# An MLP's first stage by seven products instead of eight, through DRAM, in a hybrid decoder block

## The chip, the cores and the metric

The kernel runs on one core of a Trainium2 chip. The metric is the device time of one execution in microseconds (us); lower is better. A core has TensorE (PE, matrix products; its weight loads are listed apart as PEld), VectorE (DVE), ScalarE (ACT), GpSimd (POOL) and SyncE (SP), which here issues all transfers between DRAM and the on-chip memory SBUF. Products land in PSUM, eight banks of 128 x 512 floats.

## The reference

One decoder layer over 2048 tokens of width 1024 in float32. Attention and a gated spatial mixer come first; the change touches the MLP behind them:

```python
h = _rmsnorm(x, norm_pre_mlp[layer])
a = jax.nn.relu(jnp.einsum('bsd,df->bsf', h, w_mlp_in[layer]))   # 1024 -> 4096
y = jnp.einsum('bsf,fd->bsd', a * a, w_mlp_out[layer])           # 4096 -> 1024
x = x + _rmsnorm(y, norm_post_mlp[layer])
```

## The kernel before, in words

**Precision.** Every large product is made of three matmuls. `split` (L68 to L76) turns a float32 tile into a high part, rounded to the matmul's type (on ACT, L71, or POOL, L73), and a low part, the rest (DVE, L76). `mm3` (L85 to L88) multiplies high by high, high by low and low by high into one PSUM bank. `split_in` (L78 to L83) loads by SP and then splits.

**Order.** PE's order is written out by hand (`tc.manual_schedule`, L57): it executes matmuls in the order of the program. The queues of the other engines are put in order by the framework's scheduler, from priorities in program order and when inputs are ready; each engine then executes its queue in order. SP's queue holds all transfers and is in order too: one that waits holds up those behind it. A pool of tiles with `bufs=n` under one `tag` lets a new tile be written once the n-th older one has been read for the last time.

**Before the MLP.** `out_block` (L762) works on 128 tokens: output projection, residual, two norms, and in its second part, which `flush` (L806) runs one block later, transposes of the normed rows (L799) that ACT copies (L800) and SP writes to the DRAM tensor `h2_d` (L801), laid out depth by token. The token chunks of 512 go in the order 2, 3, 0, 1, so the upper half (`half` 1) is ready first, and the MLP begins with it. The last blocks of out_block, those of chunk 1, belong to half 0. While their last flush is still to come, PE has the first two stage-1 tiles of half 1 (two calls of `mlp_in`).

**The MLP.** For each half of 1024 tokens, f runs over 32 tiles of 128 hidden channels.

- Stage 1, `mlp_in` (L842): for one f and one chunk of 512 tokens, 8 depth tiles x 3 = 24 matmuls into one bank (`a`). ACT takes the relu out of the bank (L854), POOL squares it (L855), and ACT and DVE split it into the tile `s` that stage 2 uses from SBUF.
- Weights: `load_w1` and `load_w2` load 512 KB for each f, POOL makes the high part and DVE the low one.
- Stage 2, `mlp_out` (L913): for a group of FG = 2 tiles f it goes over 8 token blocks i and 2 column halves n; each (i, n) is 2 x 3 matmuls into a bank (`y`), which DVE adds to the accumulator in SBUF (L932). A group is made up one step behind stage 1. The last group of a half takes 4 f and goes on to the final norm: ACT squares (L935), POOL multiplies by the gain (L936), DVE ends the norm (L938, `rstd_of` L90 to L104) and adds the residual (L943), SP writes the output.

Both stages alternate on PE inside one loop over f. `psum_any` deals out all eight banks in turn to `a` and `y`.

Of the kernel before, what the change touches and what calls it, by code (L numbers as in the profile page):

```python
# [8 lines left out]
F32 = mybir.dt.float32  # L9
F32R = mybir.dt.float32r  # L10
AF = mybir.ActivationFunctionType
# [5 lines left out]
P = 128  # L17
S = 2048
D = 1024
KT = 8  # L20
NF = 32
# [3 lines left out]
HALF = 1024  # L25
FG = 2
# [16 lines left out]
def block_kernel(ctx, tc, a, out):  # L43
    nc = tc.nc
    pe, act, dve, pool, sp = nc.tensor, nc.scalar, nc.vector, nc.gpsimd, nc.sync
    x = a["x"]

    def stack(es, name, bufs=1, side=None, space=None):
        kw = dict(name=name, bufs=bufs, reuse_waits="tile")
        if side:  # L50
            kw["side"] = side
        if space is not None:
            kw["space"] = space
        return es.enter_context(tc.tile_pool(**kw))
# [13 lines left out]
    def split(hi, lo, src, hi_eng="act", lo_eng="dve"):  # L68

        if hi_eng == "act":  # L70
            act.activation(hi, src, AF.Copy)  # L71
        elif hi_eng == "pool":
            pool.tensor_scalar(hi, src, 1.0, 1.0, op0=OP.mult, op1=OP.mult)  # L73
        else:
            dve.tensor_copy(hi, src)
        (pool if lo_eng == "pool" else dve).tensor_sub(lo, src, f32(hi))  # L76

    def split_in(w, src, raw=None, hi_eng="pool", lo_eng="dve"):  # L78

        if raw is None:  # L80
            raw = f32(w)[:, 1]
        sp.dma_start(raw, src)
        split(w[:, 0], w[:, 1], raw, hi_eng, lo_eng)  # L83

    def mm3(ps, lh, ll, rh, rl, start, stop):  # L85
        pe.matmul(ps, lh, rh, start=start, stop=False)  # L86
        pe.matmul(ps, lh, rl, start=False, stop=False)  # L87
        pe.matmul(ps, ll, rh, start=False, stop=stop)  # L88
# [18 lines left out]
    def dtile(shape, name):  # L107
        return dram.tile(shape, F32, name=name)
# [9 lines left out]
    yg_d = dtile([4, P, S], "ygd")  # L118
    x1_d = dtile([S, D], "x1d")
    h2_d = dtile([P, KT, S], "h2d")  # L120
    hT_d = dtile([2, P, KT, 512], "hTd")


# [157 lines left out]
    with ExitStack() as e1a:  # L281
# [6 lines left out]
        for n in range(2):  # L288
            p = psum_aux(f"busy{n}")
# [29 lines left out]
        for half in range(2):  # L319
# [343 lines left out]
    for n in range(len(units) + 1):  # L663
        u = None
# [144 lines left out]
            last[0] = None  # L809

    chunks = (2, 3, 0, 1)
    e3 = ExitStack()
    s_, w1_, w2_, hch, cnt, raws, rls = {}, {}, {}, {}, [0], {}, []
# [5 lines left out]
    def load_h(half, ci):  # L819
        if (half, ci) in hch:  # L820
            return
        c = half * 2 + ci
        h = (hB if ci else r3).tile([P, 2, KT, 512], F32R, name=f"h2T{c}", tag="h2T", bufs=1)
        for k in range(0, KT, 2):
            split_in(h[:, :, k:k + 2], h2_d[:, k:k + 2, c * 512:(c + 1) * 512], None, "act")
        hch[half, ci] = h

    def load_w1(half, f):
        if (half, f) not in w1_:
            w1_[half, f] = r3.tile([P, 2, KT, P], F32R, name=f"w1_{half}{f}", tag="w1", bufs=2)  # L830
            if (half, f) in raws:
                raw = raws.pop((half, f))
            else:
                raw = wp3.tile([P, KT, P], F32, name=f"w1r_{half}{f}", tag="wraw", bufs=2)
            split_in(w1_[half, f], a["w_mlp_in"][f], raw)

    def load_w2(half, f):
        w2_[half, f] = wp3.tile([P, 2, D], F32R, name=f"w2_{half}{f}", tag="w2", bufs=4)
        raw = wp3.tile([P, D], F32, name=f"w2r_{half}{f}", tag="wraw", bufs=2)
        split_in(w2_[half, f], a["w_mlp_out"][f], raw)  # L840

    def mlp_in(half, f, ci):  # L842

        nm = f"{half}{f}{ci}"
        h, w1 = hch[half, ci], w1_[half, f]
        if ci == 0 and f % 4 < 2:
            s = r3.tile([P, 2, 512], F32R, name=f"s_{nm}", tag="s", bufs=2)
        else:
            s = sL.tile([P, 2, 512], F32R, name=f"s_{nm}", tag="s")
        p = psum_any(f"a_{nm}")  # L850
        for k in range(KT):
            mm3(p, w1[:, 0, k, :], w1[:, 1, k, :], h[:, 0, k, :], h[:, 1, k, :], k == 0, k == KT - 1)
        t = rls.pop() if rls else tp3.tile([P, 512], F32, name=f"rl_{nm}", tag="rl", bufs=2)
        act.activation(t, p, AF.Relu)  # L854
        pool.tensor_mul(t, t, t)  # L855
        split(s[:, 0], s[:, 1], t)
        s_[half, f, ci] = s

    def spatial_out(dt):

# [17 lines left out]
    for n, c in enumerate(chunks):  # L878
        if n:
            mg = merge(c, yt, {2: flush})  # L880
        if n < 3:
            yt = load_y(chunks[n + 1])
        for i in range(4):
            b = out_block(c, i, mg)
            next(b)
            flush()
            last[0] = b
            if n == 3 and i == 1:
                e2r.close()
                r3 = stack(e3, "r3", 1, side="right")  # L890
                load_h(1, 0)
                rw = yp.tile([P, 3, KT, P], F32, name="w1r_first", tag="yt")
                for f in range(2):
                    raws[1, f] = rw[:, f]
                    rls.append(rw[:, 2, f * 4:(f + 1) * 4].rearrange("p k t -> p (k t)"))
                    load_w1(1, f)


    first_half, second_half = 1, 0
    for f in range(2):  # L900
        mlp_in(first_half, f, 0)
    flush()
    e2.close()
    wp3 = stack(e3, "wp3", 1)
    hB = stack(e3, "hB", 1)
    yp = stack(e3, "yp3", 1)
    sL = stack(e3, "sL", 6)
# [5 lines left out]
    def mlp_out(half, f0, n_f, acc):  # L913
        first, final = f0 == 0, f0 + n_f == NF
        for i in range(8):
            isl = slice((i % 4) * P, (i % 4 + 1) * P)
            t0 = half * HALF + i * P
            if final:
                x1 = tp3.tile([P, D], F32, name=f"x1_{half}{i}", tag="x1", bufs=3)
                sp.dma_start(x1, x1_d[t0:t0 + P, :])  # L920
                ss = sm.tile([P, 2], F32, name=f"fs_{half}{i}", tag="fs")
            for n in range(2):
                nsl = slice(n * 512, (n + 1) * 512)
                an = acc[i][:, nsl]
                p = psum_any(f"y_{half}{f0}{i}{n}")
                for q in range(n_f):
                    sT, w2 = s_[half, f0 + q, i // 4], w2_[half, f0 + q]
                    mm3(p, sT[:, 0, isl], sT[:, 1, isl], w2[:, 0, nsl], w2[:, 1, nsl], q == 0, q == n_f - 1)
                if first:
                    dve.tensor_copy(an, p)  # L930
                else:
                    dve.tensor_add(an, an, p)  # L932
                if final:
                    junk = tp3.tile([P, 512], F32, name=f"jk_{half}{i}{n}", tag="rl")
                    act.activation(junk, an, AF.Square, accum_out=ss[:, n:n + 1])  # L935
                    pool.tensor_mul(an, an, gfin[:, nsl])  # L936
            if final:
                dve.tensor_add(ss[:, 0:1], ss[:, 0:1], ss[:, 1:2])  # L938
                r = rstd_of(sm, ss[:, 0:1], 1, 1.0 / D, f"fin{half}{i}")
                cut = 2 if half == second_half and i == 7 else 1  # L940
                for n in range(cut):
                    nsl = slice(n * D // cut, (n + 1) * D // cut)
                    dve.scalar_tensor_tensor(x1[:, nsl], acc[i][:, nsl], r, x1[:, nsl], op0=OP.mult, op1=OP.add)  # L943
                    sp.dma_start(out[t0:t0 + P, nsl], x1[:, nsl])

    for half in (first_half, second_half):
        for ci in range(2):
            load_h(half, ci)
        acc = [yp.tile([P, D], F32, name=f"acc{half}{i}", tag=f"acc{i}") for i in range(8)]
        pending = []  # L950
        for f in range(NF):
            for ci in range(2):
                if (half, f, ci) not in s_:
                    mlp_in(half, f, ci)
            if f + 1 < NF:
                load_w1(half, f + 1)
            load_w2(half, f)
            if f % FG == FG - 1:
# [3 lines left out]
        if half == first_half:  # L962
            load_w1(second_half, 0)
        mlp_out(half, pending[0], 2 * FG, acc)
    e3.close()


# [59 lines left out]
```

## Time and profile before

| | us |
|---|---|
| median of 3 runs (lowest, highest) | 2916.16 (2915.44, 2920.83) |
| the profiled execution: its own time | 2919.46 |
| its span in the trace | 2917.7 |
| mean granted clock of PE in it | 0.993 |
| first MLP matmul, from the span's start | 1494.59 |

The profile's lines give line number, engine, operation, output and inputs, shape, count, then the busy time, the mean duration of one in ns, and the idle time before it with what ended it. A matmul's duration overlaps that of its neighbours. A window row gives, for a stretch of time, its length, the busy time of PE, PEld, DVE, ACT and POOL with the number of instructions, the granted clock of PE (1.00 is full), the busy share of the transfer engines and GB/s. A row of transfers gives the count, the size and the median time from issue to landing. A row of the timeline gives start and duration, and in brackets the idle time before it and what ended it.

### The profile page before, as it was taken

The page shows a single profiled execution, that of the slowest core. Times are in us where ns is not written, and L with a number is a line of the kernel's source. Part 1 is how long each engine was busy: PE and PEld are TensorE (multiplying, and loading weights), DVE is VectorE, ACT ScalarE, POOL GpSimd, SP SyncE. Part 2 cuts the span into 40 slices and gives each one's busy share as a digit, 9 for nine tenths or more (in the row PEclk, how much of TensorE's full clock was granted, in tenths as well). Part 3 has the DMA queues.
Part 4 walks back from the last instruction along what each step waited for, and adds up shares of the span by engine and source line. Part 5 has one row for each costly group of instructions (what it writes and reads, how often), then busy time and mean ns, then how long its engine had stood idle before and what let it go on. Part 6 is the DMA issues. An engine that isn't in the chain of part 4 may idle for free.

```text
span 2917.7 us, 36127 instructions
## 1 busy us (share of the span) xinstructions
PE 2873.2 (98%) x14132; PEld 2412.8 (83%) x14132; DVE 1424.1 (49%) x2433; ACT 695.4 (24%) x1531; POOL 589.9 (20%) x495
## 2 busy tenths in 40 slices
PE   8999999999999999899999999999999999999998
PEld 8889889888788879687888888888888888888886
DVE  5664561444443354654564444444466444444455
ACT  4213111244443322444431101101122101101102
POOL 0340340200000043111121211211224111112113
PEclk9999999999999999999999999999999999999999
DMA  7544455566666373644551111111134111111112
GB/s 252 175 146 151 154 152 162 159 216 192 207 186 195 134 226 111 212 147 143 166 188 51 52 51 44 51 45 49 51 126 141 51 44 51 51 44 51 51 36 94
DMA packets 186570, 350.56 MB, mean 120 GB/s; under 512 B 13728, under 2 KB 81568, under 8 KB 186400
## 3 DMA queue, kind: packets, MB, share of 16 engines
q1 hardware_dynamic: 186400, 348.25, 37.4%
q8 instruction: 111, 1.82, 0.3%
q14 instruction: 59, 0.48, 0.1%
HBM read 247.34 MB, written 100.86 MB: 119 GB/s over the span
## 4 chain that ended last, share of the span: by engine, by line
PE 88%; DMA 4%; DVE 3%; ACT 2%; issue 1%; POOL 1%; SPq 0%; DVEq 0%; ACTq 0%; POOLq 0%
PE a L88 8%; PE a L86 8%; PE a L87 8%; PE y L86 8%; PE y L88 8%; PE y L87 8%; PE g L86 4%; PE g L88 4%; PE g L87 4%; PE x L88 3%; PE x L87 3%; PE x L86 3%; DMA g<-gated 2%; PE pv L595 2%; PE o L86 1%
## 5 line engine op out<-in xcount | busy, mean ns | idle before, releaser
L932 DVE TENSOR_TENSOR acc<-acc,y 128x512 f32<-128x512 f32 x448 | 301.0, 685 | 214.1 <-PE y L88 213.8
L86 PE MATMUL a<-h2T,w 128*128 128x512 f32 x1024 | 401.9, 392 | 0.0
L88 PE MATMUL a<-h2T,w 128*128 128x512 f32 x1024 | 401.7, 392 | 0.1
L87 PE MATMUL a<-h2T,w 128*128 128x512 f32 x1024 | 401.4, 392 | 0.0
L86 PE MATMUL y<-w,s 128*128 128x512 f32 x1024 | 400.3, 391 | 0.0
L88 PE MATMUL y<-w,s 128*128 128x512 f32 x1024 | 400.2, 391 | 0.0
L87 PE MATMUL y<-w,s 128*128 128x512 f32 x1024 | 399.9, 391 | 0.0
L854 ACT ACTIVATE rl<-a 128x512 f32<-128x512 f32 x126 | 75.2, 597 | 948.1 <-PE a L88 948.1
L88 PEld LDWEIGHTS a<-h2T,w 128*128 128x128 f32 x1024 | 191.9, 187 | 44.9 <-DVE w L76 0.5
L87 PEld LDWEIGHTS a<-h2T,w 128*128 128x128 f32 x1024 | 191.9, 187 | 43.9
L86 PEld LDWEIGHTS a<-h2T,w 128*128 128x128 f32 x1024 | 191.9, 187 | 43.8
L87 PEld LDWEIGHTS y<-w,s 128*128 128x128 f32 x1024 | 192.1, 188 | 42.5
L88 PEld LDWEIGHTS y<-w,s 128*128 128x128 f32 x1024 | 192.1, 188 | 42.4
L86 PEld LDWEIGHTS y<-w,s 128*128 128x128 f32 x1024 | 192.1, 188 | 42.1
L76 DVE TENSOR_TENSOR w<-w1r,w 128x1024 fp32r<-128x1024 f32 x62 | 126.4, 2039 | 183.9 <-POOL w L73 183.9
L73 POOL TENSOR_SCALAR w<-w2r 128x1024 fp32r<-128x1024 f32 x64 | 67.8, 1060 | 687.3 <-PE y L88 538.2
L76 DVE TENSOR_TENSOR w<-w2r,w 128x1024 fp32r<-128x1024 f32 x64 | 104.2, 1630 | 137.7 <-POOL w L73 137.7
L855 POOL TENSOR_TENSOR rl<-rl 128x512 f32<-128x512 f32 x126 | 133.9, 1063 | 136.4 <-ACT rl L854 136.4
L76 DVE TENSOR_TENSOR s<-rl,s 128x512 fp32r<-128x512 f32 x126 | 90.5, 718 | 138.7 <-ACT s L71 138.7
L86 PE MATMUL x<-hT_a,wq 128*128 128x512 f32 x384 | 149.7, 390 | 0.0
L88 PE MATMUL x<-hT_a,wq 128*128 128x512 f32 x384 | 149.5, 389 | 0.0
L87 PE MATMUL x<-hT_a,wq 128*128 128x512 f32 x384 | 149.4, 389 | 0.0
(249 smaller groups left out, 5516.5 us busy)
## 6 DMA issues: line engine op xcount, KB each, us to landing
w2r<-in_w_mlp_out_dram SPq DMA_DIRECT2D x64, 512.0 KB, 3.5
w1r<-in_w_mlp_in_dram SPq DMA_DIRECT2D x62, 512.0 KB, 3.5
qk<-hl SPq DMA_DIRECT2D x24, 1024.0 KB, 5.3
qq<-qk SPq DMA_DIRECT2D x96, 256.0 KB, 5.0
w_g_r<-in_w_in_dram SPq DMA_DIRECT2D x32, 512.0 KB, 5.2
gated<-gt SPq DMA_DIRECT2D x64, 256.0 KB, 2.8
g<-gated SPq DMA_DIRECT2D x64, 256.0 KB, 3.8
vd<-vt SPq DMA_DIRECT2D x16, 768.0 KB, 3.5
```

The source lines that it names most:

```text
L73: pool.tensor_scalar(hi, src, 1.0, 1.0, op0=OP.mult, op1=OP.mult)
L76: (pool if lo_eng == "pool" else dve).tensor_sub(lo, src, f32(hi))
L86: pe.matmul(ps, lh, rh, start=start, stop=False)
L87: pe.matmul(ps, lh, rl, start=False, stop=False)
L88: pe.matmul(ps, ll, rh, start=False, stop=stop)
L595: pe.matmul(pv[:, o0:o0 + w_], l, r, start=n == 0, stop=n == len(mms) - 1, skip_group_check=True)
L854: act.activation(t, p, AF.Relu)
L855: pool.tensor_mul(t, t, t)
L932: dve.tensor_add(an, an, p)
```

## The change

Stage 1 is done by Strassen's algorithm in Winograd's form. Two f tiles (a pair q, 16 pairs), the two depth halves of 512 and the two token chunks of a half make a 2 x 2 block product; it takes seven block products of 4 depth tiles x 3 matmuls (`product`) in place of eight. The sums of the token operand (T1 to T4) are made once in a half by `sum_b`, on POOL and DVE, from tiles `braw` loaded from `h2_d`; those of the weights (S1 to S4) by `sum_a` on POOL for each pair, from a raw tile of 1 MB with two buffers. All of them are split. Products accumulate in three banks for each pair; ACT copies product 1 out (`xs`), DVE adds it to products 6, 7 and 4, and further adds, relu on ACT and a square on POOL give the four outputs of the pair, which SP writes to a new DRAM tensor `s_d`.

PE's order: at the start and end of a half, `ahead` and `chain` arrange 4 and 3 pairs so that products 1 and 2, which need no sums, come first; in between each pair takes 1, 6, 2, 7, 5, 4, 3. `need` asks for operands six products ahead. `sum_b` stands in the program just before the first product of the half that follows the flush.

Stage 1 of both halves comes first, then stage 2 of both halves. Stage 2 loads `s` from `s_d` (`load_s`: 256 KB for each f and chunk, split by ACT and DVE); its raw weight tile has one buffer in place of two shared ones. All groups have two f, the final ones too.

```diff
+    TERMS = {1: ("A11", "B11"), 2: ("A12", "B21"), 3: ("S4", "B22"), 4: ("A22", "T4"),
+             5: ("S1", "T1"), 6: ("S2", "T2"), 7: ("S3", "T3")}
+    NQ, LEAD, TRAIL = NF // 2, 4, 3
...
+    def sum_b(half):
+        names = ("T2", "T3", "T1", "T4", "B22")
+        w = {n: bp.tile([P, 2, 4, 512], F32R, name=f"{n}_{half}", tag=n, bufs=1) for n in names}
+        for k in range(4):
+            r = bp.tile([P, 5, 512], F32, name=f"braw_{half}{k}", tag="braw", bufs=1)
+            sp.dma_start(r[:, :4].rearrange("p (k t) c -> p k (t c)", k=2), h2_d[:, k::4, half * HALF:(half + 1) * HALF])
+            t = dict(T1=r[:, 0], T3=r[:, 1], T4=r[:, 2], B22=r[:, 3], T2=r[:, 4])
+            pool.tensor_sub(t["T1"], r[:, 1], r[:, 0])
+            dve.tensor_sub(t["T2"], r[:, 3], t["T1"])
+            dve.tensor_sub(t["T3"], r[:, 3], r[:, 1])
+            pool.tensor_sub(t["T4"], r[:, 2], t["T2"])
+            for n in names:
+                split(w[n][:, 0, k], w[n][:, 1, k], t[n], "act", "pool" if n in ("T4", "B22") else "dve")
...
+    def sum_a(half, q):
+        raw = araw.pop((half, q))
+        a11, a12, a21, a22 = (raw[:, f, k:k + 4] for f in range(2) for k in (0, 4))
+        names = ("S2", "S3", "S1", "A22", "S4")
...
+        t = dict(S1=s1, S3=a21, S2=a11, S4=a12, A22=a22)
+        pool.tensor_add(s1, a21, a22)
+        pool.tensor_sub(a21, a11, a21)
+        pool.tensor_sub(a11, s1, a11)
+        pool.tensor_sub(a12, a12, a11)
+        for n in names:
+            split(w[n][:, 0], w[n][:, 1], t[n], "act", "dve")
...
+    def product(half, q, i):
+        an, bn = TERMS[i]
+        w, h = a_.pop((half, q, an)), b_[half, bn]
+        which = {1: "a", 2: "a", 6: "b", 7: "b", 4: "b", 5: "c", 3: "c"}[i]
...
+        for k in range(4):
+            for n, (l, r) in enumerate(((0, 0), (0, 1), (1, 0))):
+                pe.matmul(p, w[:, l, k, :], h[:, r, k, :], start=i in (1, 6, 5) and not k and not n,
+                          stop=k == 3 and n == 2, skip_group_check=True)
...
+        if i == 1:
+            xs_[key] = rx.tile([P, 512], F32, name=f"xs_{nm}", tag="xs", bufs=5)
+            act.activation(xs_[key], p, AF.Copy)
...
+        elif i in (6, 7):
+            u_[half, q, i] = cp3.tile([P, 512], F32, name=f"u{i}_{nm}", tag=f"u{i}", bufs=2)
+            dve.tensor_add(u_[half, q, i], xs_[key], p)
...
-    for f in range(2):
-        mlp_in(first_half, f, 0)
+    for q, i in ((0, 1), (1, 1), (0, 2), (1, 2)):
+        product(first_half, q, i)
     flush()
...
+    for half in (first_half, second_half):
+        lead, trail = list(range(LEAD)), list(range(NQ - TRAIL, NQ))
...
+        order = [z for z in ahead(lead) if z[0] >= done] + chain(lead, [(LEAD, 1)])
+        for q in range(LEAD, NQ - TRAIL):
+            order += [(q, i) for i in (1, 6, 2, 7, 5, 4, 3) if (q, i) != (LEAD, 1)]
+        order += ahead(trail) + chain(trail, [])
...
+            for z in order[n:n + 6]:
+                need(*z)
+            if not summed:
+                sum_b(half)
+                summed = True
+            product(half, q, i)
...
+            split_in(s, s_d[f, :, t0:t0 + 512], None, "act")
...
-                if pending and f + 1 < NF:
-                    mlp_out(half, pending.pop(), FG, acc)
-                pending.append(f + 1 - FG)
...
-        mlp_out(half, pending[0], 2 * FG, acc)
+    groups = [(half, f0) for half in (first_half, second_half) for f0 in range(0, NF, FG)]
+    for n, (half, f0) in enumerate(groups):
+        if n + 1 < len(groups):
+            for f in range(FG):
+                load_w2(groups[n + 1][0], groups[n + 1][1] + f)
+                load_s(groups[n + 1][0], groups[n + 1][1] + f)
...
+        mlp_out(half, f0, acc)
```

More of the change, by code (lines that the diff above doesn't have):

```diff
@@ L859, in spatial_out, with chain, ahead @@
+    def chain(qs, between):
+        o = [(qs[0], 6)]
+        for n, q in enumerate(qs):
+            o += [(q, 5), (q, 7)] + ([(qs[n + 1], 6)] if n + 1 < len(qs) else between) + [(q, 4), (q, 3)]
+        return o
+    def ahead(qs):
+        o = [(q, 1) for q in qs]
+        for n, q in enumerate(qs):
+            o.insert(min(2 * n + 2, len(o)), (q, 2))
+        return o
     def spatial_out(dt):
```

172 lines of the change are left out of this document (106 added, 66 removed).

## The prediction

> **What bounds the kernel now.** I read the page's engine totals and its chain of waits first, then the costliest groups, then windows over the stage that is replaced.
>
> ```profile
> span 2917.7 us, 36127 instructions
> PE 2873.2 (98%) x14132; PEld 2412.8 (83%) x14132; DVE 1424.1 (49%) x2433; ACT 695.4 (24%) x1531; POOL 589.9 (20%) x495
> PE 88%; DMA 4%; DVE 3%; ACT 2%; issue 1%; POOL 1%; SPq 0%; DVEq 0%; ACTq 0%; POOLq 0%
> ...
> L86 PE MATMUL a<-h2T,w 128*128 128x512 f32 x1024 | 401.9, 392 | 0.0
> L86 PE MATMUL y<-w,s 128*128 128x512 f32 x1024 | 400.3, 391 | 0.0
> ```
>
> ```profile
> core 0: us, PE busy (x) PEld busy (x) DVE busy (x) ACT busy (x) POOL busy (x), PEclk, DMA share, GB/s
> 1600.00:2150.00 550.00, 550.00 (x2396) 449.03 (x2396) 255.42 (x299) 61.55 (x100) 104.15 (x101) 1.00 0.15 48
> 1494.50:2907.50 1413.00, 1412.72 (x6156) 1152.59 (x6153) 699.24 (x863) 197.54 (x353) 310.81 (x284) 1.00 0.20 64
> ```
>
> TensorE (PE) carries 88% of the chain. From the MLP's first matmul to its last it is busy 1412.72 of 1413.00 us at full clock, and nothing else is near full: DVE 699, POOL 311, ACT 198. So each matmul taken out is worth its spacing, and each new PE stall is lost in full. The group's mean of 392 ns is no spacing, since neighbours overlap: 550.00 us for 2396 matmuls is 0.2296 us from start to start.
>
> **What goes.** Before, stage 1 is 2 halves x 32 f x 2 chunks x 24 = 3072 matmuls. After, a pair of f tiles takes seven products of 12 (4 depth tiles x 3) in place of 96: 2 x 16 x 84 = 2688. 384 fewer x 0.2296 = **88.2 us** (392 ns would have given 150.5). Stage 2 keeps its 3072. A product lasts 2.755 us, a pair 19.3, a stage-2 group of two f 96 x 0.2296 = 22.05.
>
> The page "TensorE: Matmul & The Clock Gate", section "Back-to-back issue gap", of the Trainium skill gives two spacings for 512 columns: N / 2.4 + 2.5, an estimated 215.7 ns and so 82.8 us, near the row; and about 131 ns sustained, by which only 50.3 us would go. The trace's 229.6 ns speaks against the second.
>
> **What it adds.** Prices of the operations:
>
> ```profile
> L932 DVE TENSOR_TENSOR acc<-acc,y 128x512 f32<-128x512 f32 x448 | 301.0, 685 | 214.1 <-PE y L88 213.8
> L76 DVE TENSOR_TENSOR s<-rl,s 128x512 fp32r<-128x512 f32 x126 | 90.5, 718 | 138.7 <-ACT s L71 138.7
> L76 DVE TENSOR_TENSOR hl<-r,hl 128x512 fp32r<-128x512 f32 x48 | 56.7, 1181 | 18.2 <-ACT hl L71 15.8
> L76 DVE TENSOR_TENSOR w<-w2r,w 128x1024 fp32r<-128x1024 f32 x64 | 104.2, 1630 | 137.7 <-POOL w L73 137.7
> L76 DVE TENSOR_TENSOR w<-w1r,w 128x1024 fp32r<-128x1024 f32 x62 | 126.4, 2039 | 183.9 <-POOL w L73 183.9
> L71 ACT ACTIVATE s<-rl 128x512 fp32r<-128x512 f32 x126 | 79.8, 633 | 195.9 <-POOL rl L855 195.9
> L855 POOL TENSOR_TENSOR rl<-rl 128x512 f32<-128x512 f32 x126 | 133.9, 1063 | 136.4 <-ACT rl L854 136.4
> L936 POOL TENSOR_TENSOR acc<-acc,gfin 128x512 f32<-128x512 f32 x32 | 42.4, 1337 | 56.8 <-ACT jk L935 56.8
> ```
>
> ```profile
> w1r<-in_w_mlp_in_dram SPq DMA_DIRECT2D x62, 512.0 KB, 3.5
> qk<-hl SPq DMA_DIRECT2D x24, 1024.0 KB, 5.3
> v<-vd SPq DMA_DIRECT2D x9, 1024.0 KB, 5.8
> ```
>
> *Steady stage 1 (18 pairs).* Per 19.3 us: DVE seven lows and five adds from PSUM, 7 x 0.72 + 5 x 0.69 = 8.5 (11.7 with lows at 1.18); ACT 12 x 0.63 = 7.6; POOL four sums and four squares, 8 x 1.06 = 8.5 (10.7 at 1.34); one 1 MB load and four 256 KB writes. All are beside PE. The tight loop is that S4's low part frees the raw weights, a 1 MB load follows (5.3 to 5.8), then A11's high part, ACT's copy of product 1, product 2: I count about 2 us of slack. Two products of one bank always have one other (2.755) between them, against 0.69 for the add. I take 4 us in all, 0 to 15.
>
> On the DVE spread the page "SBUF — State Buffer" of the Trainium skill, section "Who interferes with whom", says that a DVE instruction with two SBUF inputs contends with a GpSimd one that reads SBUF, the later being fully blocked. The 718 and 1181 ns of one shape would fit; no row here separates the cause.
>
> *Entry.* The token sums (T1 to T4) are loaded behind the last flush in program order: their buffers lie in memory that `e2.close()` frees, and SP's queue is in order, so they go behind the last write of h2 (of the other half), which stood in no one's way before:
>
> ```profile
> 1494.59 0.47 PE L86 MATMUL a<-h2T,w 128*128 128x512 f32 x1
> ...
> 1506.39 0.48 PE L86 MATMUL a<-h2T,w 128*128 128x512 f32 x1
> ...
> 1510.61 0.38 SPq L801 DMA_DIRECT2D h2d<-h  x1
> ```
>
> Count from 1494.59. 48 matmuls (11.0) and the first eight transposes of the flush reach to 1506.39, so eight transposes cost 0.8. PE has products 1 and 2 of four pairs (8 x 2.755 = 22.0), 16 transposes (1.6) and three quarters of product 6 (2.1): it is out of work at 25.7. (Pairs 2 and 3 come later than that, behind the first sums on ACT and SP; the wait for T2 covers it.) The first `braw` load is queued on SP behind the 1510.61 write, at 16.3. `braw` has one buffer, so the four depth steps go in series: issue and load 5.7, POOL's T1 1.34, DVE's T2 0.69, POOL's T4 1.34, ACT's high part 0.63, POOL's two low parts 2.68 (they free the buffer): 12.4. I take POOL at the 1.34 it has beside a busy DVE; at 1.06 it is 11.2. The fourth load is issued at 16.3 + 3 x 12.4 = 53.5 and lands at 58.8; T1, T2 and T2's split end 3.4 later, 62.2. POOL's weight sums for the first pairs stand between: 4 x 1.34 = 5.4 for one, half of it under the loads, 2.7. T2 is ready at 64.9, and PE waits 64.9 - 25.7 = **39 us** (29 with a 9.5 step and no sums between; 47 with a 13.5 step and two pairs).
>
> *Middle (half 1 to 0).* The T tiles are single too, so their new values wait for half 1's last products; PE covers with the same 24.7 us of products 1 and 2. The second load is issued 2.1 after the last product, the fourth at 2.1 + 24.8 = 26.9, lands at 32.2; 3.4 gives 35.6; one pair's sums 5.4: 41.0. **16 us** (3 to 24).
>
> *Ends of the halves.* The last three pairs run without other pairs between: an add queued behind the low parts of the next pair's sums costs some 2.2, two neighbours in one bank 1. 3.2 x 2 = **6.5** (2 to 12).
>
> *Clock.* After idle PE stretches the granted clock fell:
>
> ```profile
> 798.70:805.50 6.80, 2.47 (x12) 1.62 (x10) 5.06 (x6) 5.40 (x12) 0.00 (x0) 0.91 0.88 330
> 805.50:810.00 4.50, 4.50 (x17) 3.81 (x17) 0.69 (x1) 0.60 (x1) 0.00 (x0) 0.50 0.81 216
> 1075.00:1082.00 7.00, 2.60 (x12) 1.91 (x11) 1.90 (x2) 0.60 (x1) 6.92 (x3) 0.91 0.74 222
> 1082.00:1090.00 8.00, 8.00 (x29) 6.62 (x28) 3.18 (x2) 1.79 (x3) 1.54 (x2) 0.65 0.19 70
> ```
>
> 4.5 us at 0.50 lose 2.3, 8.0 at 0.65 lose 2.8. After the two long stalls: **5** (3 to 8).
>
> *Stage 2.* s goes through DRAM, 32 MB out and back, some 50 GB/s where 64 flow now. Per group DVE has 16 adds, two weight lows and four s lows: 16 x 0.69 + 2 x 1.63 + 4 x 0.72 = 17.2 of 22.05 (19.8 with lows at 1.18 and 2.04); buffers for s and w2 leave 3 to 5 us for their loads. No cost. The first group's loads cost 1 (0 to 6).
>
> *The final groups.* They now merge two f, not four, so PE takes 2.76 us for an i where it took 5.5, and DVE's chain shows:
>
> ```profile
> 2902.82 1.28 DVE L932 TENSOR_TENSOR acc<-acc,y 128x512 f32<-128x512 f32 x2
> 2904.97 0.73 DVE L938 TENSOR_TENSOR fs<-fs 128x1 f32<-128x1 f32 x1 [0.87 <-ACT jk L935]
> ...
> 2906.26 0.68 DVE L99 SCALAR_TENSOR_TENSOR t_fin<-r_fin,v_fin 128x1 f32<-128x1 f32 x1
> ...
> 2907.42 1.28 DVE L943 SCALAR_TENSOR_TENSOR x<-acc,r_fin,x 128x1024 f32<-128x1024 f32 x1
> 2908.62 1.28 DVE L932 TENSOR_TENSOR acc<-acc,y 128x512 f32<-128x512 f32 x2
> ...
> 2913.17 1.41 DVE L943 SCALAR_TENSOR_TENSOR x<-acc,r_fin,x 128x512 f32<-128x512 f32 x2
> ...
> 2862.80:2917.70 54.90, 44.48 (x194) 36.05 (x192) 36.22 (x74) 14.51 (x42) 21.34 (x17) 0.93 0.35 125
> ```
>
> From 2902.82 to 2908.62 is 5.8 us, about 1 of it waiting for ACT: DVE needs 4.8. Eight i are 38.5, and from the end of the last chain (2914.6) to the span's end 3.1 more: 41.6. The last two groups then take 22.05 + 41.6 = 63.7, where the last row has 54.9 for the same four f: **9** (5 to 16). In half 1 the same 38.5 plus the next group's splits, 6.1, make 44.6 against 22.05 of PE and the 11 that eight banks let PE run ahead: **11** (3 to 20).
>
> *Sum.* 39 + 16 + 6.5 + 5 + 4 + 1 + 9 + 11 = 91.5 less 88.2: +3.3 on the profiled execution's own 2919.5, which is 3.3 above the median of the runs. 2919.5 + 3.3 - 3.3: I forecast **2919**, gain and stalls cancelling. Its own range, with half of each bound's distance, is 2900 to 2942.
>
> **Rivals.** *Short starts (faster).* The price of both starts hangs on one step, the `braw` period. If 1 MB lands in 3.5 us, as 512 KB do, and POOL keeps 1.06, a step is 0.4 + 3.5 + 1.06 + 0.69 + 1.06 + 0.63 + 2.1 = 9.5. The fourth load is then issued at 44.8 and T2 ready near 51.5 (26 us of stall), and in the middle at 27.8 (3). 26 fewer: **2893**. It decides below a step of about 10.9, where the total falls 10 under the forecast. For it: DMA is quiet at that point of the MLP. Against: every 1 MB row says 5.3 or more, and POOL has another pair's sums in hand.
>
> *Loop beyond its slack (slower).* If a 1 MB load beside the writes lands 7.8 us after issue, 2 us are lost in each of the 18 steady pairs: +36, **2955**. It decides at 7.4. For it: one raw buffer chain with 2 us of slack; against: 5.3 to 5.8.
>
> *DVE bound in stage 2 (slower).* If the adds too stretch, to 0.95, beside POOL's splits, a group is 16 x 0.95 + 4 x 1.18 + 2 x 2.04 = 24, and 2 us over 32 groups are +64: **2983**. It decides at 22.05. For it: DVE's lows of one shape differ by a factor of 1.6; against: the adds read PSUM and mean 685 over 448.
>
> *The matmuls spaced otherwise.* A gain of 50.3 as in the second spacing above would give 2957; the windows leave little room for it. That fewer products are saved I give no chance: the loops count them.
>
> **Chances.** Forecast 0.56, short starts 0.20, loop 0.11, DVE bound 0.10, other spacing or a mishap 0.03. 0.2% is 5.8 us, about what a measurement of this kernel can tell from no change. Within the forecast's range I put 0.15 below 2910, 0.18 between 2910 and 2922, 0.23 above. Faster 0.15 + 0.20 = 0.35; same 0.18; slower 0.23 + 0.11 + 0.10 + 0.03 = 0.47. The range for 8 in 10, 2886 to 2962, takes in the short starts and the loop and leaves out DVE bound and the farthest bounds.
>
> **What would show it.** In the profile after: 2688 matmuls into the banks of stage 1, a pair in 19.3 us in the middle of a half, and 22.05 for a stage-2 group; a PE gap of 39 us ending in T2's low part some 26 us after the first product, with four loads 12.4 apart; a gap of 16 at the half's change; 11 at the first half's final group; a tail 9 longer. I am wrong if those gaps are half as long, if steady pairs exceed 19.5, or if DVE is above 95% in stage 2.

## The result, and the profile after

The changed kernel takes 2953.94 us (median of 4 runs, 2950.71 to 2957.38) against 2916.10 for the kernel before, a ratio of 1.0126 (95% interval 1.0108 to 1.0145): 1.3% slower. Its profiled execution took 2956.97 us with a span of 2955.3, so the two profiled spans differ by 37.6 us. The changed kernel also sets `dynamic_dma_scratch_size=2048` where the program is made, which the part on the change does not list; no run tries it apart.

The page of the changed kernel, engine totals and the costliest groups:

```profile
span 2955.3 us, 37242 instructions
PE 2805.8 (95%) x13748; PEld 2357.8 (80%) x13748; DVE 1626.4 (55%) x2817; ACT 863.8 (29%) x1819; POOL 768.4 (26%) x591
...
L893 PE MATMUL ab<-T,S 128*128 128x512 f32 x768 | 191.9, 401 | 50.3 <-ACT T L71 37.9
...
L893 PE MATMUL aa<-B,A 128*128 128x512 f32 x768 | 189.0, 401 | 24.0 <-ACT A L71 16.6
```

PE has 14132 - 13748 = 384 instructions fewer, as counted, and is busy 67 us less; but it is 95% busy where it was 98%. The last column of the groups shows idle time ahead of the matmuls, which was 0.0 before: 50.3 us ahead of the group of products that read T and S, 37.9 of them ended by T's high part on ACT, and 24.0 ahead of products 1 and 2, 16.6 of them ended by the high part of the weights.

The windows of the changed kernel, cut where PE's order has its sections: entry (nine products and the flush), lead of half 1 with its first steady pair (26 products), its other steady pairs and trail (77), the same three for half 0 after the middle, then stage 2 in groups 1 to 15, 16 to 18 (half 1's last is the 16th), 19 to 30, and the last two with the end:

```profile
core 0: us, PE busy (x) PEld busy (x) DVE busy (x) ACT busy (x) POOL busy (x), PEclk, DMA share, GB/s
1491.55:1569.89 78.34, 33.67 (x119) 24.56 (x118) 43.51 (x45) 26.23 (x48) 46.02 (x32) 0.67 0.44 154
1569.89:1652.14 82.25, 75.79 (x314) 61.04 (x312) 48.67 (x57) 27.23 (x46) 45.45 (x34) 0.94 0.36 115
1652.14:1871.44 219.30, 213.05 (x925) 174.40 (x924) 106.14 (x134) 82.86 (x135) 102.30 (x82) 0.99 0.40 137
1871.44:1925.39 53.95, 28.86 (x110) 22.60 (x109) 30.22 (x26) 19.83 (x35) 41.71 (x31) 0.77 0.44 146
1925.39:2002.79 77.40, 73.98 (x313) 60.30 (x312) 46.27 (x55) 27.39 (x46) 42.45 (x32) 0.96 0.34 109
2002.79:2219.43 216.64, 212.78 (x925) 174.43 (x924) 103.39 (x130) 75.80 (x126) 104.80 (x85) 0.99 0.38 127
2219.43:2547.37 327.94, 327.94 (x1442) 270.38 (x1441) 225.51 (x330) 39.84 (x63) 30.83 (x31) 1.00 0.33 103
2547.37:2626.33 78.96, 71.31 (x290) 56.82 (x288) 71.11 (x122) 20.87 (x52) 34.03 (x23) 0.94 0.57 187
2626.33:2888.73 262.40, 262.40 (x1154) 216.31 (x1153) 181.35 (x264) 30.31 (x48) 25.12 (x25) 1.00 0.31 97
2888.73:2955.30 66.57, 43.89 (x193) 35.86 (x191) 51.88 (x94) 14.83 (x42) 24.93 (x18) 0.87 0.34 119
```

Fifteen undisturbed groups (1440 matmuls) take 327.94 us: 0.2277 a matmul. (A steady pair takes 19.15 us, from 1652.14 to 1671.29, which is 84 matmuls at that rate.) The loss of a section is its length less its matmuls at that rate:

| section | matmuls | loss, us | foreseen |
|---|---|---|---|
| entry, with its slow clock (0.8 of transposes taken off) | 108 | 52.9 | 41.5 |
| lead with the first steady pair, half 1 and half 0 | 312 + 312 | 11.2 + 6.4 | in the 4 of the next row |
| the seven inner steady pairs of each half | 588 + 588 | 0 | 4 for all 18 |
| last steady pair and trail, half 1 and half 0 | 336 + 336 | 8.9 + 6.2 | 6.5 |
| middle, with its slow clock | 108 | 29.4 | 18.5 |
| start of stage 2 | | 0 | 1 |
| groups 16 to 18 | 288 | 13.4 | 11 |
| last two groups and end | 192 | 22.9; in the kernel before 11.6 in its whole MLP, some 10.7 of it in its last four f | 9 more |

So 115.0 in stage 1, 13.4 and 11.3 (22.9 less 11.6) in stage 2 are lost, 139.7 in all. Against it stand 384 x 0.2296 = 88.2 for the matmuls that went, 5760 x 0.0019 = 10.9 since the others stand 0.2277 apart and not 0.2296, and 3.0 since stage 1 began at 1491.55 and not 1494.59: 102.1. The difference is the 37.6 us of the spans.

PE in the entry (timeline of the changed kernel: start, duration, then the idle time before and what ended it):

```profile
1491.55 11.15 PE L893 MATMUL aa<-B,A 128*128 128x512 f32 x48
...
1520.13 1.22 PE L893 MATMUL aa<-B,A 128*128 128x512 f32 x2 [16.55 <-ACT A L71]
...
1539.11 2.96 PE L893 MATMUL ab<-T,S 128*128 128x512 f32 x6 [3.61 <-ACT S L71]
1553.37 0.79 PE L893 MATMUL ab<-T,S 128*128 128x512 f32 x1 [11.30 <-ACT T L71]
...
1566.66 0.80 PE L893 MATMUL ab<-T,S 128*128 128x512 f32 x1 [9.85 <-ACT T L71]
```

and in the middle:

```profile
1897.59 5.49 PE L893 MATMUL aa<-B,A 128*128 128x512 f32 x12 [6.90 <-ACT xs L905]
...
1922.15 0.79 PE L893 MATMUL ab<-T,S 128*128 128x512 f32 x1 [16.77 <-ACT T L71]
```

The low part of T2's last quarter lets PE go at 1568.87, one wait of 1.42 us after the last row of the entry. That is some 77 us after the first product; 65 was foreseen. In the middle, the product at 1897.59 takes 5.28 us until the next one starts at 1902.87, 0.44 for each of its 12 matmuls; the granted clock in these 5.28 us is 0.50. By the page "TensorE: Matmul & The Clock Gate", section "Back-to-back issue gap", of the Trainium skill, throttled matmuls of N = 512 columns stand N / 1.2 ns apart, an estimated 427; the trace agrees.

What held T back stands on POOL (timeline of the changed kernel; the T row is the end of the second depth step, L844 the start of the third):

```profile
1533.65 1.74 POOL L76 TENSOR_TENSOR T<-braw,T 128x512 fp32r<-128x512 f32 x1
...
1549.18 1.70 POOL L844 TENSOR_TENSOR braw<-braw 128x512 f32<-128x512 f32 x1
```

From 1535.39 to 1549.18 stand 13.8 us of other work, without a gap: seven weight sums of two pairs (L875 to L877, L874) and two squares (L897). The loads of `braw` on SP were issued at

```profile
1507.21 0.55 SPq L842 DMA_DIRECT2D braw<-h2d  x1
...
1521.28 0.55 SPq L842 DMA_DIRECT2D braw<-h2d  x1
...
1536.01 0.52 SPq L842 DMA_DIRECT2D braw<-h2d  x1
...
1557.27 13.81 SPq L842 DMA_DIRECT2D braw<-h2d  x2
```

that is, steps of 14.1, 14.7 and 21.3 us, where 12.4 were foreseen for each. (The second load of the last row is the other half's first.)

### The profile page after: what moved, and what is told of

It is laid out like the page before. It is cut to its first block, busy times and chain, and to the rows that moved or that the text cites. A ratio compares the mean times of both kernels' runs of the same rounds, so it can differ in the third digit from the quotient of the medians.

```text
span 2955.3 us, 37242 instructions
## 1 busy us (share of the span) xinstructions
PE 2805.8 (95%) x13748; PEld 2357.8 (80%) x13748; DVE 1626.4 (55%) x2817; ACT 863.8 (29%) x1819; POOL 768.4 (26%) x591
## 5 line engine op out<-in xcount | busy, mean ns | idle before, releaser
L71 ACT ACTIVATE s<-s 128x512 fp32r<-128x512 f32 x128 | 80.6, 632 | 561.6 <-DMA s<-sd 530.7
L893 PE MATMUL ab<-T,S 128*128 128x512 f32 x768 | 191.9, 401 | 50.3 <-ACT T L71 37.9
L88 PEld LDWEIGHTS y<-w,s 128*128 128x128 f32 x1024 | 193.1, 189 | 41.9
L893 PEld LDWEIGHTS ab<-T,S 128*128 128x128 f32 x768 | 147.2, 193 | 86.1 <-ACT T L71 39.8
L893 PE MATMUL aa<-B,A 128*128 128x512 f32 x768 | 189.0, 401 | 24.0 <-ACT A L71 16.6
L897 POOL TENSOR_TENSOR c<-c 128x512 f32<-128x512 f32 x126 | 146.6, 1165 | 215.2 <-ACT c L917 184.7
L893 PEld LDWEIGHTS aa<-B,A 128*128 128x128 f32 x768 | 147.8, 193 | 58.0 <-ACT A L71 16.8
L73 POOL TENSOR_SCALAR w_g<-w_g_r 128x1024 fp32r<-128x1024 f32 x32 | 33.6, 1049 | 413.1 <-PE g L88 331.0
L76 DVE TENSOR_TENSOR A<-w1r,A 128x512 fp32r<-128x512 f32 x92 | 92.6, 1015 | 86.1 <-ACT A L71 85.6
L76 DVE TENSOR_TENSOR s<-s 128x512 fp32r<-128x512 f32 x128 | 88.6, 694 | 72.0 <-ACT s L71 71.8
L893 PE MATMUL ab<-T,A 128*128 128x512 f32 x384 | 96.4, 402 | 10.6 <-DVE u L912 10.6
```

The costliest lines, as they stand in the source:

```text
L893: pe.matmul(p, w[:, l, k, :], h[:, r, k, :], start=i in (1, 6, 5) and not k and not n, stop=k == 3 and n == 2, skip_group_check=True)
```

## The experiments

Theory 1: T comes late since POOL makes token sums and weight sums in one queue, and the raw buffer is single. Theory 2: the lead and trail sections lose time since the next raw weights are loaded behind writes of s in SP's queue. Theory 3: the final groups are bound by DVE. The losses quoted below are made as in the table above, with 0.2277 us a matmul, from each run's own trace. They come from one trace each, and sections that an edit does not touch differ too: the lead of half 1 loses 11.2 in the change, 8.7 in e4 and 8.3 in e9. The MLP's first matmul stands anywhere from 1488.4 to 1497.2 us in these traces, for reasons not looked into, so a few us between two totals need not be an edit's.

**e1: half 0 without its own token sums.**

```diff
-            if not summed:
+            if not summed and half == second_half:
+                for m in ("T2", "T3", "T1", "T4", "B22"):
+                    b_[half, m] = b_[first_half, m]
+                summed = True
```

> Half 0 uses half 1's token sums T1 to T4 and B22 again, so sum_b does not run in the middle (half 0's stage 1 is computed from the wrong tokens; only the time is of interest). Theory 1: the 29 us lost between the last product of half 1 and product 5 of half 0 are the wait for T2, so they fall to under 5, some 2928 us in all. Rival: a good part is the wait of product 1 for its bank and weights (the 6.9 us before the wait for T2), which stays with its slow clock: 10 or more remain, 2936.

One run: 2933.46 us. The window of the middle:

```profile
1869.13:1900.50 31.37, 26.72 (x109) 21.29 (x108) 11.21 (x11) 10.39 (x19) 18.79 (x16) 0.95 0.43 142
```

31.37 for the nine products that took 53.95: 6.8 lost in place of 29.4. So the token sums are the cause of 22.6 of the middle's 29.4. The 6.8 lie between the two numbers expected. They are the rival's kind of wait: in e1's trace PE waits 1.27 and 3.37 us there for ACT's copy of product 1 (`xs`), and matmuls are slow behind it.

**e2: the sums moved from POOL to DVE.**

```diff
-            pool.tensor_sub(t["T1"], r[:, 1], r[:, 0])
+            dve.tensor_sub(t["T1"], r[:, 1], r[:, 0])
...
-            pool.tensor_sub(t["T4"], r[:, 2], t["T2"])
+            dve.tensor_sub(t["T4"], r[:, 2], t["T2"])
...
-        pool.tensor_add(s1, a21, a22)
...
+        eng = dve if q < LEAD else pool
+        eng.tensor_add(s1, a21, a22)
...
```

> Token sums T1 and T4 on DVE in place of POOL, and the weight sums of the first four pairs of each half on DVE too; POOL keeps the low parts of T4 and B22. Theory 1: POOL is what holds T2 back, since the weight sums of two pairs and two squares (13.8 us) stand in its queue between the second and third depth step. Then the steps become 11 to 12 us, T2's last quarter is ready some 62 us after the first product in place of 77, and the middle gains the same way: 20 to 25 us less, about 2930. Rival A: the single raw buffer and the 6 us of each load set the step; the steps stay near 13 and only the 7 us of queueing go in each half, about 2940. Rival B: DVE, which gets 4 x 0.7 more a step and 4 more a pair, becomes late itself; the lead sections lose what the entry gains, 2950 or more.

2927.81 us, ratio to before 1.0036 (1.0022 to 1.005): 26 us less than the change. SP's loads of `braw` in its timeline:

```profile
1506.86 0.55 SPq L842 DMA_DIRECT2D braw<-h2d  x1
...
1547.30 12.56 SPq L842 DMA_DIRECT2D braw<-h2d  x2
```

The three steps take 40.4 us where they took 50.1, 13.5 each: the long one is gone, but they are not 11 or 12. The windows of the entry and of the middle:

```profile
1491.20:1558.07 66.87, 31.61 (x120) 23.12 (x119) 45.62 (x65) 26.33 (x48) 15.93 (x12) 0.72 0.53 181
1852.79:1896.17 43.38, 28.28 (x110) 21.62 (x109) 36.15 (x44) 19.52 (x35) 16.95 (x13) 0.85 0.54 181
```

The entry loses 41.5 (52.9 in the change) and the middle 18.8 (29.4). The time is the one that theory 1 named, the step length that of rival A: the move off POOL was worth 11 in each half, and what is left is a step of 13.5 us with its load in series. Rival B did not come: the leads lose 7.1 and 6.3.

**e3: the writes of s issued by POOL.**

```diff
-            sp.dma_start(s_d[f, :, half * HALF + ci * 512:half * HALF + (ci + 1) * 512], t)
+            pool.dma_start(s_d[f, :, half * HALF + ci * 512:half * HALF + (ci + 1) * 512], t)
```

> The writes of s are issued from POOL's queue, right behind the squares, in place of SP's. Theory 2: in the lead and trail sections the next raw weights are loaded late because their load stands in SP's queue behind writes of s that wait for squares; those sections lose 11 + 9 + 6 + 6 = 32 us beside the waits for T, and that falls to 12 or less: about 2934. Rival: the cycle of a raw buffer (load 5 to 6, four sums of 1.3 to 1.7, splits) is 16 us by itself, more than the 13.7 of five products, and no time is won; within 4 us of 2954. A cost of issuing from POOL would show as longer squares or gaps on POOL in the steady pairs.

2943.53 us, ratio 1.009 (1.0075 to 1.0105): 10 us less than the change. In the change's lead, SP and POOL stand so (timelines):

```profile
1610.32 0.39 SPq L862 DMA_DIRECT2D w1r<-in_w_mlp_in_dram  x1
1611.39 14.77 SPq L898 DMA_DIRECT2D sd<-c  x3
1626.25 0.39 SPq L862 DMA_DIRECT2D w1r<-in_w_mlp_in_dram  x1
```

```profile
1624.33 1.49 POOL L897 TENSOR_TENSOR c<-c 128x512 f32<-128x512 f32 x1
```

The square ends at 1625.82, the write that waits for it follows, and behind that the load at 1626.25: 15.9 us after the load before it, where a lead pair takes PE 13.7. The lateness reaches PE through DVE's queue: low parts of such weights start there at 1633.46, and behind them, at 1637.80, comes the add (`u`, L912) for which PE waits 3.38 us. The lead's window in e3:

```profile
1570.94:1643.48 72.54, 72.42 (x313) 59.21 (x312) 50.36 (x57) 27.83 (x46) 52.29 (x48) 0.98 0.38 127
```

72.54 for the 26 products that took 82.25: 1.5 lost. Of the two leads' 17.6 us 5.0 are left (1.5 and 3.5), and half 1's trail loses 4.5 in place of 8.9; but the last steady pair and trail of half 0 lose 10.6 in place of 6.2. So theory 2 holds for the leads and half of one trail and not for half 0's end, which no run took apart. (e5, which ends half 0 alike, has low parts of stage 2's first weights in DVE's queue ahead of the add that PE waits 3.12 us for; that they are the cause is not shown.) POOL's own queue shows no cost in the inner steady pairs, which take 19.15 us here too.

**e4: half 0's last two groups as one of four f.**

```diff
+        fs = range(f0 - FG if final and half == second_half else f0, f0 + FG)
...
-                for q in range(FG):
...
+                for f in fs:
...
+        if half == second_half and f0 == NF - 2 * FG:
+            continue
         mlp_out(half, f0, acc)
```

> Half 0's last two groups are merged again into one of four f, as in the kernel before. Theory 3: the tail was 9 us longer since PE took 2.7 us for a token block where DVE needs 4.8; with 5.5 us of PE a block DVE keeps up and the end comes 9 to 10 us earlier, about 2944. Rival: the wait is elsewhere in the end (x1 loads, writes), and it is less than 4 us.

2953.54 us (2945.99 to 2955.11), no difference from the change that the medians show. But in its trace the MLP starts at 1497.16, 5.6 us later than in the change, so the total does not price the end. The end takes 61.8 us from the start of the same four f, 4.8 less than 66.57, and not the 9 to 10 expected. Lines of DVE's timeline, of which the last two are each the pair of additions of one token block, show what was misread:

```profile
2898.71 1.23 DVE L76 TENSOR_TENSOR w<-w2r,w 128x1024 fp32r<-128x1024 f32 x1 [2.55 <-POOL w L73]
2901.25 0.69 DVE L1073 TENSOR_TENSOR acc<-acc,y 128x512 f32<-128x512 f32 x1 [1.31 <-PE y L88]
...
2926.62 1.28 DVE L1073 TENSOR_TENSOR acc<-acc,y 128x512 f32<-128x512 f32 x2
...
2932.43 1.28 DVE L1073 TENSOR_TENSOR acc<-acc,y 128x512 f32<-128x512 f32 x2
```

A block takes 5.81 us, as it did in the kernel before (5.80), and PE's four f take 24 x 0.2277 = 5.46: in this order DVE, with its waits for ACT inside a block, was the bound before too. And the last group's weights are split only at 2898.71, since their buffers are those of the group two before; the first addition comes 10 us after the group's start, and PE waits 4.79 us there for the weights' high part.

**e5: six lead pairs**, with e2 and e3 in it.

```diff
-    NQ, LEAD, TRAIL = NF // 2, 4, 3
+    NQ, LEAD, TRAIL = NF // 2, 6, 3
...
-            return rls.pop() if rls else cp3.tile([P, 512], F32, name=f"{name}_{nm}", tag="c", bufs=6)
+            return rls.pop() if rls else cp3.tile([P, 512], F32, name=f"{name}_{nm}", tag="c", bufs=4)
...
-            xs_[key] = rx.tile([P, 512], F32, name=f"xs_{nm}", tag="xs", bufs=5)
+            xs_[key] = rx.tile([P, 512], F32, name=f"xs_{nm}", tag="xs", bufs=7)
```

> The sums on DVE and the writes on POOL's queue together, and six lead pairs in place of four (seven xs tiles; four c tiles in place of six make room). Alone the two edits took 26 and 10 us, so 2918 without the lead. Theory 1: T2 is ready when its chain of loads and sums ends, whatever PE does meanwhile; two more lead pairs put four products (10.9 us) in front of the wait in each half, and 15 to 22 us more go: 2896 to 2903. Rival: the two pairs' weights (two more loads of 1 MB on SP, eight more splits, eight more DVE sums) stand in T2's way and push it back as far: 2912 or more.

2896.84 us, ratio 0.9934 (0.992 to 0.9949): faster than the kernel before. Its windows of the entry and of the middle (13 products each now), and PE's waits in stage 1 (total, times, longest):

```profile
1492.88:1557.15 64.27, 43.22 (x167) 33.00 (x166) 41.87 (x60) 29.48 (x54) 23.31 (x17) 0.83 0.65 219
...
1832.97:1879.52 46.55, 38.55 (x158) 30.99 (x156) 37.11 (x39) 22.62 (x41) 23.82 (x23) 0.89 0.58 198
```

```profile
PE aa L894 <- ACT A L71: 13.6, 1, 13.6
PE aa L894 <- ACT xs L906: 8.0, 2, 7.4
...
PE ab L894 <- ACT T L71: 2.4, 1, 2.4
```

The entry loses 64.27 - 156 x 0.2277 - 0.8 = 27.9, the middle 11.0. The wait for T, 37.9 us in the change, is 2.4; what is left in the entry is the third pair's weights and the slow clock behind that gap. T's last quarter lets PE go 63.3 us after the first product, 65.9 in e2: the two pairs did not push it back, as theory 1 had it, and the rival falls.

**e6: two raw buffers for the token sums**, four lead pairs, with e2 and e3 in it.

```diff
-            r = bp.tile([P, 5, 512], F32, name=f"braw_{half}{k}", tag="braw", bufs=1)
+            r = bp.tile([P, 5, 512], F32, name=f"braw_{half}{k}", tag="braw", bufs=2)
...
```

> The same two edits with four lead pairs and two raw buffers for the token sums in place of one (room from c 6 to 4, wl 7 to 6, s1 2 to 1). Theory 1a: of a step of 13.5 us the load is 6.3, which now lies beside the sums of the step before; steps of 7 to 8, T2 ready some 17 us earlier in each half: 2918 - 30 = 2888, the entry losing about 25 us and the middle under 8. Rival: DVE and POOL, not the load, are full in this stretch, and the steps stay above 11: 2908 or more. A cost of the smaller pools would show as losses in the steady pairs, where none are now.

To make room, `c` goes from 6 buffers to 4, `wl` from 7 to 6 and `s1` from 2 to 1. 2908.91 us, ratio 0.9976 (0.9966 to 0.9985). PE's waits in its stage 1:

```profile
PE aa L894 <- ACT A L71: 20.2, 1, 20.2
PE ab L894 <- DVE u L913: 14.8, 6, 5.3
...
PE ab L894 <- ACT T L71: 1.8, 1, 1.8
```

The wait for T is gone here too (37.9 to 1.8), the entry loses 30.2 and the middle 6.2. But the high parts of the third pair's weights stand on ACT behind the token splits of two steps now (20.2 in place of 16.6), and the ends of the halves lose more than in e3 (8.3 and 15.5 where it lost 4.5 and 10.6), with waits for u on DVE. The loads of `braw` in half 1 are issued 7.5 us apart on average, as expected; the total is at the rival's number for another reason. Whether the smaller pools or the earlier transfers cost the rest was not separated.

**e7: both.** e5's and e6's edits together, and one more for room:

```diff
-            u_[half, q, i] = cp3.tile([P, 512], F32, name=f"u{i}_{nm}", tag=f"u{i}", bufs=2)
+            u_[half, q, i] = cp3.tile([P, 512], F32, name=f"u{i}_{nm}", tag=f"u{i}", bufs=1)
```

> Lead of six and two raw buffers together (u tiles single too, for room). If the wait for T2 is all that is left in the entry and the middle, what remains there is the wait for the weights of the third pair (15 us) and the slow clock: 2870 to 2880. If the smaller pools bind, u's single buffer above all, the lead and trail sections and the steady pairs lose, and it is no better than the better of the other two.

2899.26 us, ratio 0.9942 (0.9928 to 0.9957): no better than e5, the second of the two outcomes expected. In its trace no wait for T's high part is left, where e5 had 2.4 us, so the second buffer had little to win; the wait for the weights' high part is 21.0 us where it was 13.6, and the waits for u are 10.2 where they were 5.2. Which of the smaller pools costs that was not separated.

**e8: the two phases with plain products.** Stage 1 is made of 24 matmuls a tile again, without sums:

```diff
+    def direct(half, q, f, ci):
+        p = psum_any(f"d_{half}{q}{f}{ci}")
+        for kk in range(2):
+            w, h = a_[half, q, f"A{f + 1}{kk + 1}"], b_[half, f"B{kk + 1}{ci + 1}"]
+            for k in range(4):
+                mm3(p, w[:, 0, k, :], w[:, 1, k, :], h[:, 0, k, :], h[:, 1, k, :], not kk and not k, kk == 1 and k == 3)
...
```

> Stage 1 in eight plain products (3072 matmuls as in the kernel before), everything else as in the change: s through DRAM, the two stages in separate phases, final groups of two f. Theory 3: the separation costs what the final groups show, 13 in the first half's end and 10 to 12 more in the last, and nothing else: 6144 matmuls at 0.228 to 0.2296 us, 2930 to 2940 in all, and so Strassen with all its waits costs another 15 to 25. Rival: the round trip through DRAM or the loads of B12 and B22 stall PE in places where the sums now hide it: 2950 or more.

2953.68 us, ratio 1.0131 (1.0114 to 1.0148): the same time as the change, and the rival's number. Its windows of the first four tiles and of the first group of stage 2:

```profile
1489.63:1521.40 31.77, 26.19 (x107) 20.72 (x106) 16.50 (x27) 14.82 (x25) 3.12 (x3) 0.89 0.81 268
2206.78:2236.79 30.01, 25.31 (x96) 19.88 (x97) 20.21 (x28) 5.92 (x10) 4.62 (x5) 0.83 0.63 214
```

The final groups cost what was expected (13 in half 1, 12 more at the end), but 9.1 us (9.9 with the transposes) are lost behind the flush, where PE waits 5.6 for splits of the second chunk's tokens, and 8.2 in the first group of stage 2, where it waits for weights and s: such stalls were the rival's. The second does not exist in the change (its fifteen first groups lose nothing). So this run is no pure measure of the phases. What it shows is that the arrangement without Strassen takes as long as with it: in the traces stage 1 lasts 717.2 us with plain products and 727.9 with seven, so the 88 us of matmuls are given back in the waits of stage 1.

**e9: the final norm for four token blocks at once**, on the change as it is.

```diff
-                ss = sm.tile([P, 2], F32, name=f"fs_{half}{i}", tag="fs")
+                if i % 4 == 0:
+                    ss = sm.tile([P, 2, 4], F32, name=f"fs_{half}{i}", tag="fs")
...
+            if final and i % 4 == 3:
+                dve.tensor_add(ss[:, 0], ss[:, 0], ss[:, 1])
+                r = rstd_of(sm, ss[:, 0], 4, 1.0 / D, f"fin{half}{i}")
...
```

> The change as it is, with the final norm made for four token blocks at once (one chain of small DVE operations for four columns, then four residual operations). Theory 3: the final groups lose time because DVE needs 4.8 us a block against 2.73 of PE. Now it needs (8 x 0.69 + 1 + 4 x 1.28) / 4 = 2.9: the 13 us lost around half 1's final group fall to 4 or less, and the end, 41.9 us from the start of the last group, to some 32: about 20 less, 2934. Rival: POOL (two products with the gain, 2.7 us a block) or its contention with DVE holds the pace near 4; 8 us or less are won.

2944.05 us, ratio 1.0107 (1.009 to 1.0124): 10 less, half of what was expected. (The 41.9 us of the expectation run from the last group's second addition; from its first matmul it is 44.8.) Its windows of groups 16 to 18 and of the last two with the end:

```profile
2541.30:2614.39 73.09, 67.88 (x290) 55.08 (x288) 65.43 (x88) 18.46 (x46) 31.97 (x23) 0.98 0.56 202
2876.79:2939.00 62.21, 43.89 (x193) 35.87 (x191) 43.11 (x60) 13.00 (x36) 22.30 (x18) 0.89 0.30 110
```

5.9 and 4.4 less than in the change, with DVE 5.7 and 8.8 less busy. The 10 lie between the 20 of theory 3 and the 8 of the rival: the norm's small operations on DVE were part of what is lost there, and what POOL's products cost was not separated. The run also gives `x1` five buffers in place of three, and in the change the last residual waits 1.02 us for its load of `x1`, so a part of the 4.4 can be that.

**e10 and e11: the parts together.** e10 is e5 with e9; e11 loads 512 KB where a lead or trail pair needs only its first f tile:

```diff
-                load_a(half, q)
+                load_a(half, q, 1 if part == 1 and (q < LEAD or q >= NQ - TRAIL) else 2)
```

> Lead of six, sums on DVE, writes on POOL's queue (2896.8 together) and the norm in fours. If the parts add, 2877; 2885 or more if the norm in fours meets something that only this arrangement has.

> The same, and where a lead or trail pair needs only its first f tile (products 1 and 2), 512 KB are loaded in place of 1 MB. If the transfers that run beside the token loads in the entry slow them (6.3 us a load where 5.3 was expected), each step shrinks by up to 1 us and the third pair's weights come earlier: 3 to 6 us less than the run before it. If the order on ACT sets it, within 2 us.

e10: 2889.20 us, ratio 0.9911 (0.9896 to 0.9926). e11: 2889.44 us, 0.9916 (0.9901 to 0.993). The parts add nearly (2887 from the medians of e5 and e9; the 2877 expected counted on 20 us from e9), so the second branch of e10's expectation has the number and not the reason. The smaller loads win nothing, as expected if ACT's order sets it: in e11 the third pair's product still waits 12.9 us for its weights' high part, which stands on ACT behind the token splits.

## Why the prediction was right or wrong

The forecast was 2919 with 2886 to 2962 for 8 in 10; the time is inside that range and 35 above the number, and 12 above the 2942 that ended the forecast's own range. That the wide range holds it is partly luck: its upper end was set by a rival that did not happen. The prediction said that gain and stalls cancel; they do not, with 139.7 us lost where 91.5 were foreseen. The kinds of stall were mostly right, their sizes too small, and one was missing. By its steps:

- **The gain.** 384 matmuls at 0.2296 was right, and 10.9 us came on top, which no step had, since the spacing itself fell from 0.2296 to 0.2277. The rival of another spacing had no part.
- **Entry.** Right in kind: PE runs out of work there and goes on with T2's low part. It is not one gap of 39 us but seven, 44.7 in all, the first of them 16.55 for the third pair's weights, which the prediction had covered by the wait for T2. Mis-sized, 52.9 against 41.5. The step failed in "POOL's weight sums for the first pairs stand between ... half of it under the loads, 2.7": 13.8 us stood there in one piece, of which the landing of the third load (5.6 us) hid less than half. The step of 12.4 was short as well: 13.5 without that piece (e2). Of the 16 transposes that it counted, the traces have eight behind the first product, 0.8 us less of work.
- **Middle.** The same term, 29.4 against 18.5; e1 puts 22.6 of it down to the token sums, and the move off POOL in e2 takes 10.6.
- **Lead sections.** Missing. "I count about 2 us of slack" was counted for pairs of 19.3 us, and there it held: the seven inner steady pairs of each half lose nothing. A lead pair has only 13.7 us of PE left, against a raw-weight cycle near 16. The prediction listed the four writes of each pair but did not follow SP's queue, where the next load stands behind them; e3 shows some 13 of the 17.6 us to be that.
- **Ends of the halves.** 15.1 against 6.5. SP's queue is a part of half 1's (it falls to 4.5 in e3); half 0's rises to 10.6 there, and its cause is open.
- **Stage 2.** Right: groups of 21.9 us without a loss through DRAM, no cost at its start, 13.4 around half 1's last group against 11, and 66.6 us for the last two groups and the end against 63.7. That the old end of 54.9 was set by PE was wrong in part: its blocks of 5.8 us were DVE's too (e4).
- **The clock.** Each of the two gaps was given 2.5. In the entry 52.9 less the 44.7 that PE sat idle in the timeline leaves 8, in the middle 29.4 less 25.1 leaves 4. The term was too small for the entry, which has several gaps with slow matmuls behind them: the 46 from 1521.86 on take 13.64 us, 0.297 each.
- **The rivals.** "Short starts" had the sign wrong: steps are longer, not shorter. "Loop beyond its slack" gave 2955, the time that came, for a reason that did not: the inner steady pairs lose nothing, and their 1 MB loads land after some 5.1 us. Its price was off too, since by the 2 us of slack a landing of 7.8 would have cost a pair at most 0.5. DVE is not bound in stage 2's ordinary groups: it is busy 225.5 of 327.9 us in the first fifteen.

## What to carry to other kernels

Where one engine takes over two streams of preparation (here token sums and weight sums), what counts at the start of a phase is the queue of that engine, in order, with all that is ready by then, not the sum of one stream; write it out per step. A slack counted in the steady loop says nothing for the sections at its ends, where the same loads have less matmul time to hide behind; and a load that shares an in-order queue with stores waits for what the stores wait for. More independent work ahead of a late operand (e5) took the wait for it away as fully as a shorter chain did (e6), and here it cost less elsewhere.

## What the runs showed of the hardware

Matmuls of one shape stand 0.2296 us apart in the kernel before and 0.2277 in the changed one, and within a steady pair it goes by product (timeline of the changed kernel):

```profile
1652.14 2.92 PE L893 MATMUL aa<-B,A 128*128 128x512 f32 x12
1654.90 2.89 PE L893 MATMUL ab<-T,S 128*128 128x512 f32 x12
...
1663.13 2.88 PE L893 MATMUL ac<-T,S 128*128 128x512 f32 x12
1665.85 2.88 PE L893 MATMUL ab<-T,A 128*128 128x512 f32 x12
```

Product 1 takes 2.76 us from start to start, product 5 takes 2.72. The products of one shape thus differ by 1 to 2% in pace; they read different tiles and write different banks, and what in that sets it was not tried.

DVE's smallest operations took up to six times their time while POOL was busy. Two lines of the same operation in half 1's last group:

```profile
2561.62 1.26 DVE L99 SCALAR_TENSOR_TENSOR t_fin<-r_fin,v_fin 128x1 f32<-128x1 f32 x1
...
2587.41 0.21 DVE L99 SCALAR_TENSOR_TENSOR t_fin<-r_fin,v_fin 128x1 f32<-128x1 f32 x1
```

One element a partition takes 1.26 us in the first and 0.21 in the second. POOL runs two products with the gain from 2560.55 to 2564.12, over the whole of the first, and nothing from 2586.41 to 2594.14, around the second. The page "SBUF — State Buffer", section "Who interferes with whom", of the Trainium skill has it that of a two-input DVE instruction and a GpSimd instruction that reads SBUF the later is blocked for the whole of the other; the two lines agree with that, though no run took POOL's work away to show the cause.
